# Hybrid diffusion layer on one core: query evictions by pairs, earlier loads of the cached keys and values, another list of attention stages, and the query norm applied inside the exponential

## The chip, the core and the metric

One core of a Trainium2 chip runs the whole program. The metric is the device time of one execution in microseconds (us). The kernel before takes 767.54 us, the median of three runs (766.51 to 768.29).

## What is computed

One layer of a backbone with two streams: 512 latent tokens (four tiles of 128) and 128 context tokens (a fifth tile). Everything is float32; an accurate product is made of three passes on rounded high and low parts.

```python
h = _rms(x, norm_mix) * (1 + sc1) + sh1            # adaLN from SiLU(cond) @ w_ada
q, k, v, gb, gc, u = split(h @ w_in)               # 8 query heads, 2 key heads, head_dim 64
q = _rms(q, q_norm); k = _rms(k, k_norm)           # per head
# latent tokens: rotary on q and k, keys = cached context keys + latent keys (640)
sc = einsum("bqkgd,btkd->bkgqt", q, k) * HEAD_DIM ** -0.5
attn = softmax(sc) @ v
y_conv = gb * conv3(gc * u)
x = x + g1 * (concat(_rms(attn), _rms(y_conv)) @ w_out)
x = x + g2 * ((silu(gate) * up) @ w_down)          # adaLN, then SwiGLU
```

## The kernel before, in words

The program has four stretches. In the first (to about 62 us) the inputs are normalised and transposed, the modulation is computed, and the query columns of the projection are accumulated for all five token tiles in five PSUM banks. In the second (to about 263 us) keys and values are projected and normalised, attention runs, and the convolution mixer is computed as filler between the steps of attention. The third is the output projection, the fourth (from about 335 us) the feed-forward network.

TensorE runs in the order in which the code is written. That order comes from two lists of short words. `P1SEQ` is the first stretch: `d8` is eight throw-away 128x128 matmuls (`spin`, L509) that only keep TensorE busy, `r`/`s`/`x` are norm, scale and transposes of an input tile, `q70` adds step 7, the last, of the query projection for tile 0, `E0` is the eviction of that tile's accumulator by ScalarE (`q_evict`, L581; tile 4, the context, by VectorE). Within `P1SEQ` the other engines also run in written order, with their priorities. Two query tiles share one PSUM tile of two banks: 0 and 1 the first, 2 and 3 the second. A write of the second half waits for any read of the first half that was written before it in the program.

`SEQ` is the second stretch. `k1` is the key/value projection of tile 1 with its head norm, `K1` the transposes of the keys, `c0`/`C0` the same for the cached keys and values (they need no projection), `q0`/`Q0` head norm and transposes of the queries, `a0`/`t0`/`o0` scores and softmax, transposes, and output of the context tile's head group 0, `S5.1` the scores and softmax of the second head of unit 5 (a unit is one latent tile, one key head and one pair of its query heads; 16 units, 32 head-scores), `T5.0` transposes of its probabilities, `O5.0` the product with the values, and `F1` one step of the convolution filler: 9, 9 and 6 matmuls of 320 columns in turn (L703 to L705), sometimes a step of the modulation (L387). The other engines' order in this stretch is set by a scheduler with priorities; within an engine it is strict.

The head norm of queries (`head_norm`, L605) squares (ScalarE L610), sums (VectorE L612), raises to the power -1/2 on GpSimd (L164), multiplies the factor by 1/8 on VectorE (L166), applies gain and rotary (L617 to L628), and multiplies the 512 columns by the factor (L629). The split into a high part (ScalarE L674) and a low part (VectorE L675) comes after that.

A head-score (`att_s`, L811): four matmuls of 320 columns into the only scores tile in PSUM (L817), the negated row maximum on VectorE (L821), the exponential with that maximum as its bias and the row sum as second output on ScalarE (L825), then reciprocal (L828) and scaling by VectorE (L832) or ScalarE (L830). The next head-score can't start before the exponential has read the tile. `ctx_s` (L890) does four heads of the context tile at once.

The loads of the first stretch are issued by SyncE in the order of the string `LOADS`: `x` an input tile, `A` three steps of modulation weights, `W` a block of the projection's weights. The loads of the cached keys and values, `ck` and `cv` (L366, L367), stand behind all of them. The weights rotate through three buffers, so SyncE waits for a buffer in the middle of the list.

Of the kernel before, what the change touches and what calls it, by code (L numbers as in the profile page):

```python
# [9 lines left out]
F32 = mybir.dt.float32  # L10
F32R = mybir.dt.float32r
AF = mybir.ActivationFunctionType
ALU = mybir.AluOpType
AX = mybir.AxisListType

P = 128
# [3 lines left out]
NT = 5  # L20
TOK = NT * P
CTX = 4
HD = 64
NH = 8
NKV = 2
GRP = NH // NKV
# [3 lines left out]
NKEY = 640  # L30
EPS = 1e-6
CG = 32
P1SEQ = ('d8 r0 s0 x0 r1 s1 r2 e00d x1 s2 e01d r3 v0 d4 x2 s3 e20a a0 e10d b0 e11d e21d x3 m0 d4 w e30a h00y l n0 '
# [4 lines left out]
XB = 3  # L38
SEQ = ('k1 c0 q4 k4 C0 k0 K4 F1 Q4 q0 a0 F1 k2 a1 K0 t0 k3 t1 o0 K1 F1 Q0 o1 F1 K2 F1 K3 F1 F1 S0.0 F1 S0.1 '
# [10 lines left out]
GCUT = [0, 6, 12, 17, 22]  # L50
GB = 3
SOP = [20, 0]
# [31 lines left out]
AHEAD = 3  # L84
OSQ = 2
AFB = 4
LOADS = 'xxxxAWxAAWAAWAAAWWWWW'
O_Q, O_K, O_GB, O_GC, O_U = 0, 512, 768, 1280, 1792


def build(ctx, tc, x_prompt, x_sample, c, cache_k, cache_v, c_ctx, norm_mix, norm_ffn, w_ada, b_ada,
# [27 lines left out]
    def T(tag, shape, dt=F32, bufs=1):  # L119
        seq[0] += 1  # L120
        return pools[where.get(tag, "A")][1].tile(list(shape), dt, tag=tag, bufs=bufs, name=f"{tag}_{seq[0]}")
# [33 lines left out]
        pe.matmul(out, lh, rl, start=False, stop=False, skip_group_check=more)  # L155
        pe.matmul(out, ll, rh, start=False, stop=stop, skip_group_check=more)  # L156

    def rstd_of(ss, n, scale, extra=None, tag="rs"):

        w = ss.shape[1]  # L160
        ms = T("ms", (P, w), F32, 4)
        dve.tensor_scalar(ms, ss, scale, EPS, ALU.mult, ALU.add)
        r = T(tag, (P, w), F32, 6)
        pool.tensor_tensor(r, ms, neghalf[:, :w], ALU.pow)  # L164
        if extra is not None:
            dve.tensor_scalar_mul(r, r, extra)  # L166
        return r

    open_pool("A", "left", "")
# [81 lines left out]
    def load_next(later=False):  # L251
        load(order[stream_at[0]], later)
        stream_at[0] += 1
# [104 lines left out]
    for a in LOADS:  # L358
        if a == "A":
            ada1_next(3)  # L360
        elif a == "W":
            load_next(True)
        else:
            x_load()
    ck, cv = (T(x, (P, NKV, HD)) for x in ("ck", "cv"))
    sp.dma_start(ck, cache_k[0, 0])  # L366
    sp.dma_start(cv, cache_v[0, 0])  # L367
    ones = T("ones", (P, P))
    dve.memset(ones, 1.0)
    neghalf = T("neghalf", (P, 16))  # L370
# [214 lines left out]
             "n": h_rest, "E": q_evict, "R": lambda i: rope_tables()}  # L585
    in_pre[0] = True
    for x in P1SEQ.split():
        k = int(x[1:2] or 0)
        if x[0] == "h":
            h_do(k, int(x[2]), len(x) > 3)  # L590
        elif x[0] == "q":
            q_mm(k, int(x[2]))
        elif x[0] == "e":
            xT_evict(k, int(x[2]), x[3])
        else:
            steps[x[0]](k)
# [5 lines left out]
    close_pool("psum")  # L602
    open_psum("pp2", {"t": PT, "c": 5 - PT, "o": 1, "s": 1})

    def head_norm(ps, nh, t, which):  # L605

        w = nh * HD
        p3 = ps.rearrange("p (h d) -> p h d", d=HD)
        sq = T("ph", (P, 512), F32, PHB)[:, :w]
        act.activation(sq, ps, AF.Square)  # L610
        ss = T("hq_ss", (P, NH), F32, 2)[:, :nh]
        dve.tensor_reduce(ss, sq.rearrange("p (h d) -> p h d", d=HD), AX.X, ALU.add)  # L612
        r = rstd_of(ss, nh, 1.0 / HD, HD ** -0.5 if which == 0 else None)
        m1 = T("pr", (P, 512), F32, PRB)[:, :w]
        m13 = m1.rearrange("p (h d) -> p h d", d=HD)
        if t == CTX:
            dve.tensor_tensor(m13, p3, gains[which].unsqueeze(1).to_broadcast([P, nh, HD]), ALU.mult)  # L617
        else:
            cg, sg = tabs[which]
            dve.tensor_tensor(m13, p3, cg[:, t].unsqueeze(1).to_broadcast([P, nh, HD]), ALU.mult)  # L620
            m2 = T("pl", (P, 512), F32, PHB)[:, :w]
            p5 = ps.rearrange("p (h a b c) -> p h a b c", a=2, b=2, c=16)
            m5 = m2.rearrange("p (h a b c) -> p h a b c", a=2, b=2, c=16)
            s5 = sg[:, t].rearrange("p (a b c) -> p a b c", a=2, b=2)
            for b in range(2):
                dve.tensor_tensor(m5[:, :, :, b], p5[:, :, :, 1 - b],
                                  s5[:, :, b].unsqueeze(1).to_broadcast([P, nh, 2, 16]), ALU.mult)
            dve.tensor_tensor(m1, m1, m2, ALU.add)  # L628
        dve.tensor_tensor(m13, m13, r.unsqueeze(2).to_broadcast([P, nh, HD]), ALU.mult)  # L629
        return m13  # L630

# [151 lines left out]
    rB = [None] * NT  # L783
# [27 lines left out]
    def att_s(u, h):  # L811
        t, v, p = u[0:3]
        q = qT[t][:, v * GRP + 2 * p + h, :]
        s2 = PS2()
        for i, kk in enumerate((KA, KB)):
            for g in range(2):
                pe.matmul(s2[:, g, :320], q, kk[:, v, P + g * 320:P + (g + 1) * 320], start=(i == 0), stop=(i == 1))  # L817
        s_in = s2[:, :, :320]
        nm = T("nm", (P, 1), F32, 4)
        with early(SOON):  # L820
            dve.tensor_reduce(nm, s_in, AX.XY, ALU.max, negate=True)  # L821
        pr = T("pr", (P, NKEY), F32, PRB)
        sm = T("sm", (P, 1), F32, 4)
        with early(SOON):
            act.activation(pr.rearrange("p (a b) -> p a b", a=2), s_in, AF.Exp, bias=nm, accum_out=sm)  # L825
        rsm = T("rsm", (P, 1), F32, 4)
        with early(SOON):
            dve.reciprocal(rsm, sm)  # L828
            if NA[h]:
                act.activation(pr, pr, AF.Copy, scale=rsm)  # L830
            else:
                dve.tensor_scalar_mul(pr, pr, rsm)  # L832
        u[3].append(pr)
# [56 lines left out]
    def ctx_s(v):  # L890
# [7 lines left out]
        pr = T("pr", (P, NKEY), F32, PRB)[:, :512].rearrange("p (h k) -> p h k", k=P)  # L898
        with early(SOON):
            dve.tensor_reduce(nm, s3, AX.X, ALU.max, negate=True)  # L900
            for h in range(GRP):
                act.activation(pr[:, h], s3[:, h], AF.Exp, bias=nm[:, h:h + 1], accum_out=sm[:, h:h + 1])
            dve.reciprocal(rsm, sm)
            dve.tensor_tensor(pr, pr, rsm.unsqueeze(2).to_broadcast([P, GRP, P]), ALU.mult)
        cu[v] = pr
# [444 lines left out]
```

## Time and profile before

| | |
|---|---|
| median of three runs | 767.54 us |
| the profiled execution's own time | 768.41 us |
| its span, first to last instruction | 766.6 us |
| TensorE matmul busy | 746.0 us (97%) |
| VectorE busy | 554.0 us (72%) |
| ScalarE busy | 368.2 us (48%) |
| GpSimd busy | 43.7 us (6%) |

How to read it: PE is TensorE's matmul row, PEld its weight loads, DVE VectorE, ACT ScalarE, POOL GpSimd, SP SyncE with its DMA queue. In a timeline row stand the start and the duration in us, the engine, the line, the operation, output <- input by the program's names, and in brackets the idle time of that engine just before and what ended it. The ends of matmuls are modelled, so back-to-back matmuls overlap in the rows and their distance from start to start is what one costs. PEclk is the granted share of TensorE's clock in a stretch.

### The profile page before, as it was taken

The page shows a single profiled execution, that of the slowest core. Times are in us where ns is not written, and L with a number is a line of the kernel's source. Part 1 is how long each engine was busy: PE and PEld are TensorE (multiplying, and loading weights), DVE is VectorE, ACT ScalarE, POOL GpSimd, SP SyncE. Part 2 cuts the span into 40 slices and gives each one's busy share as a digit, 9 for nine tenths or more (in the row PEclk, how much of TensorE's full clock was granted, in tenths as well). Part 3 has the DMA queues.
Part 4 walks back from the last instruction along what each step waited for, and adds up shares of the span by engine and source line. Part 5 has one row for each costly group of instructions (what it writes and reads, how often), then busy time and mean ns, then how long its engine had stood idle before and what let it go on. Part 6 is the DMA issues. An engine that isn't in the chain of part 4 may idle for free.

```text
span 766.6 us, 11914 instructions
## 1 busy us (share of the span) xinstructions
PE 746.0 (97%) x4612; PEld 668.3 (87%) x4612; DVE 554.0 (72%) x1005; ACT 368.2 (48%) x713; POOL 43.7 (6%) x75
## 2 busy tenths in 40 slices
PE   7998989999999999999899999999999999999997
PEld 6677878889999887899898789998889998899986
DVE  5656876785665798779979778884577866778653
ACT  5355756666555634675552225553125541255410
POOL 2402200111000110100000000000000000000000
PEclk9999999999999999999999999999999999999999
DMA  9985133432342364030245313133113232222312
GB/s 290 288 232 158 40 113 110 150 94 90 110 152 88 127 227 137 1 111 28 84 120 169 109 56 109 57 111 110 56 55 91 76 111 71 67 84 83 110 56 82
DMA packets 101390, 84.52 MB, mean 110 GB/s; under 512 B 3503, under 2 KB 81651, under 8 KB 101333
## 3 DMA queue, kind: packets, MB, share of 16 engines
q1 hardware_dynamic: 100980, 83.39, 35.4%
q0 software_dynamic: 352, 0.37, 0.3%
q8 instruction: 36, 0.59, 0.3%
q14 instruction: 22, 0.17, 0.1%
HBM read 79.68 MB, written 2.75 MB: 108 GB/s over the span
## 4 chain that ended last, share of the span: by engine, by line
PE 83%; DVE 7%; ACT 4%; DMA 3%; issue 2%; POOL 1%; SPq 0%; DVEq 0%; POOLq 0%
PE pf L156 17%; PE pf L155 17%; PE pf L154 17%; PE pc L703 3%; PE pc L704 3%; PE pc L705 3%; PE po L860 3%; PE ph L154 2%; PE ph L156 2%; PE ph L155 2%; PE ps L817 2%; PE pc L387 2%; PE pt L843 2%; DMA es<-t 1%; PE ps L154 1%
## 5 line engine op out<-in xcount | busy, mean ns | idle before, releaser
L150 ACT ACTIVATE wh<-wf 128x512 fp32r<-128x512 f32 (+1 forms) x68 | 55.6, 818 | 81.5 <-PE pf L156 69.4
L156 PE MATMUL pf<-wh,gT 128*128 128x512 f32 (+1 forms) x225 | 88.3, 393 | 0.0
L155 PE MATMUL pf<-wl,gT 128*128 128x512 f32 (+1 forms) x225 | 87.7, 390 | 0.0
L154 PE MATMUL pf<-wh,gT 128*128 128x512 f32 (+1 forms) x225 | 87.6, 389 | 0.0
L703 PE MATMUL pc<-hH,wh 128*128 128x320 f32 x192 | 62.1, 323 | 0.4 <-ACT g L766 0.2
L705 PE MATMUL pc<-hH,wl 128*128 128x320 f32 x192 | 60.1, 313 | 0.0
L704 PE MATMUL pc<-hL,wh 128*128 128x320 f32 x192 | 59.9, 312 | 0.0
L151 DVE TENSOR_TENSOR wl<-wf,wh 128x1024 fp32r<-128x1024 f32 (+1 forms) x34 | 39.4, 1159 | 27.0 <-ACT wh L150 22.1
L155 PEld LDWEIGHTS pf<-wl,gT 128*128 128x128 f32 x225 | 42.2, 188 | 10.3 <-issue 0.2
L154 PEld LDWEIGHTS pf<-wh,gT 128*128 128x128 f32 x225 | 42.2, 188 | 9.9 <-ACT wh L150 0.2
L154 PE MATMUL pf<-T,wh 128*128 128x320 f32 x160 | 49.6, 310 | 1.1 <-ACT p L1180 0.6
L156 PEld LDWEIGHTS pf<-wh,gT 128*128 128x128 f32 x225 | 42.3, 188 | 9.3
L156 PE MATMUL pf<-T,wh 128*128 128x320 f32 x160 | 49.4, 309 | 0.0
L154 PE MATMUL pf<-T,wl 128*128 128x320 f32 x160 | 49.4, 309 | 0.0
L155 PE MATMUL pf<-T,wl 128*128 128x320 f32 x160 | 49.4, 309 | 0.0
L155 PE MATMUL pf<-T,wh 128*128 128x320 f32 x160 | 49.4, 309 | 0.0
L156 PE MATMUL pf<-T,wl 128*128 128x320 f32 x160 | 49.4, 309 | 0.0
L154 PE MATMUL pf<-B,wl 128*128 128x320 f32 x152 | 47.1, 310 | 0.0
L156 PE MATMUL pf<-B,wl 128*128 128x320 f32 x152 | 47.0, 309 | 0.0
L155 PE MATMUL pf<-B,wl 128*128 128x320 f32 x152 | 46.9, 309 | 0.0
L1259 DVE TENSOR_TENSOR dm<-pf,g 128x512 f32<-128x512 f32 (+1 forms) x41 | 27.7, 676 | 23.6 <-PE pf L156 23.5
L154 PE MATMUL pf<-B,wh 128*128 128x320 f32 x136 | 42.2, 310 | 1.5 <-DVE cu L1209 1.5
(304 smaller groups left out, 2051.3 us busy)
## 6 DMA issues: line engine op xcount, KB each, us to landing
wf<-in_w_gate_up_dram SPq DMA_DIRECT2D x44, 512.0 KB, 3.9
aw<-in_w_ada_dram SPq DMA_DIRECT2D x24, 512.0 KB, 4.1
wf<-in_w_down_dram SPq DMA_DIRECT2D x20, 512.0 KB, 3.3
wf<-in_w_in_dram SPq DMA_DIRECT2D x18, 512.0 KB, 5.2
af<-in_w_ada_dram SPq DMA_DIRECT2D x32, 256.0 KB, 6.6
x<-in_x_sample_dram SPq DMA_DIRECT2D x8, 512.0 KB, 5.7
wf<-in_w_out_dram SPq DMA_DIRECT2D x8, 512.0 KB, 4.1
wf<-in_w_ada_dram SPq DMA_DIRECT2D x8, 512.0 KB, 3.7
```

What stands on the lines that cost most here:

```text
L150: act.activation(hi, src, AF.Copy)
L151: dve.tensor_tensor(lo, src, f32(hi), ALU.subtract)
L154: pe.matmul(out, lh, rh, start=start, stop=False, skip_group_check=more)
L155: pe.matmul(out, lh, rl, start=False, stop=False, skip_group_check=more)
L156: pe.matmul(out, ll, rh, start=False, stop=stop, skip_group_check=more)
L387: pe.matmul(out[CG * g:CG * (g + 1)], cp[:, k], w, start=(k < 4), stop=(k >= KD - 4), skip_group_check=True)
L703: pe.matmul(acc, wh[:, k], hH[k][:, c0:c0 + n], start=(k == 0), stop=False)
L704: pe.matmul(acc, wh[:, k], hL[k][:, c0:c0 + n], start=False, stop=False)
L705: pe.matmul(acc, wl[:, k], hH[k][:, c0:c0 + n], start=False, stop=(k == KD - 1))
L817: pe.matmul(s2[:, g, :320], q, kk[:, v, P + g * 320:P + (g + 1) * 320], start=(i == 0), stop=(i == 1))
L860: pe.matmul(ov, w, x[:, i].rearrange("p a q -> p (a q)"), start=(g == 0 and i == 0 and n == 0), stop=(last and i == len(kts) - 1 and n == 1))
L1259: dve.tensor_tensor(dm, ps[:, :n], g2[cc][:, oc], ALU.mult)
```

## The change

1. The first word `d8` of `P1SEQ` becomes `d11`.
2. Evictions by pairs: two query accumulations, then their two evictions.
3. `ck` and `cv` are issued behind the fourth block of projection weights instead of behind the eighth.
4. The query norm factor is no longer multiplied into the query. The scores are taken with the unnormalised query (gain and rotary applied), and the exponential gets the factor as its scale. The 1/8 goes into the mean and the epsilon (`scale * by`, `EPS * by` with `by` = 64). The row maximum has to be multiplied by the factor too: one ScalarE copy of 128x1 for each head-score, one VectorE product of 128x4 for each context group. The factors of a tile live in `rq`.
5. Another `SEQ`: three of the fillers in front of the first head-score move, one to behind it and two to behind units 9 and 14. Words and their number are the same (84 fillers); the order of the other words is the same.

```diff
-P1SEQ = ('d8 r0 s0 x0 r1 s1 r2 e00d x1 s2 e01d r3 v0 d4 x2 s3 e20a a0 e10d b0 e11d e21d x3 m0 d4 w e30a h00y l n0 '
+P1SEQ = ('d11 r0 s0 x0 r1 s1 r2 e00d x1 s2 e01d r3 v0 d4 x2 s3 e20a a0 e10d b0 e11d e21d x3 m0 d4 w e30a h00y l n0 '
...
-         'm7 h70 h71 q60 q61 w l q62 q63 q64 w l q70 E0 q71 E1 q72 E2 q73 E3 q74 E4 w l')
+         'm7 h70 h71 q60 q61 w l q62 q63 q64 w l q70 q71 E0 E1 q72 q73 E2 E3 q74 E4 w l')
...
-SEQ = ('k1 c0 q4 k4 C0 k0 K4 F1 Q4 q0 a0 F1 k2 a1 K0 t0 k3 t1 o0 K1 F1 Q0 o1 F1 K2 F1 K3 F1 F1 S0.0 F1 S0.1 '
+SEQ = ('k1 c0 q4 k4 C0 k0 K4 Q4 q0 a0 F1 k2 a1 K0 t0 k3 t1 o0 K1 F1 Q0 o1 K2 F1 K3 F1 S0.0 F1 F1 S0.1 '
...
-LOADS = 'xxxxAWxAAWAAWAAAWWWWW'
+LOADS = 'xxxxAWxAAWAAWAAAWCWWWW'
...
-    def rstd_of(ss, n, scale, extra=None, tag="rs"):
+    def rstd_of(ss, n, scale, by=1.0, tag="rs"):
...
-        dve.tensor_scalar(ms, ss, scale, EPS, ALU.mult, ALU.add)
-        r = T(tag, (P, w), F32, 6)
+        dve.tensor_scalar(ms, ss, scale * by, EPS * by, ALU.mult, ALU.add)
+        r = T(tag, (P, w), F32, {"rB": 1, "rs": 6}.get(tag, NT))
         pool.tensor_tensor(r, ms, neghalf[:, :w], ALU.pow)
-        if extra is not None:
-            dve.tensor_scalar_mul(r, r, extra)
...
+        elif a == "C":
+            ck, cv = (T(n, (P, NKV, HD)) for n in ("ck", "cv"))
+            sp.dma_start(ck, cache_k[0, 0])
+            sp.dma_start(cv, cache_v[0, 0])
...
-        r = rstd_of(ss, nh, 1.0 / HD, HD ** -0.5 if which == 0 else None)
+        r = rstd_of(ss, nh, 1.0 / HD, *((HD, "rq") if which == 0 else ()))
...
+        if which == 0:
+            rq[t] = r
+            return m13
         dve.tensor_tensor(m13, m13, r.unsqueeze(2).to_broadcast([P, nh, HD]), ALU.mult)
...
-            dve.tensor_reduce(nm, s_in, AX.XY, ALU.max, negate=True)
+            dve.tensor_reduce(nm[:, 0:1], s_in, AX.XY, ALU.max, negate=True)
+            act.activation(nm[:, 1:2], nm[:, 0:1], AF.Copy, scale=rs)
...
-            act.activation(pr.rearrange("p (a b) -> p a b", a=2), s_in, AF.Exp, bias=nm, accum_out=sm)
+            act.activation(pr.rearrange("p (a b) -> p a b", a=2), s_in, AF.Exp, bias=nm[:, 1:2], scale=rs, accum_out=sm)
...
+            rs = rq[CTX][:, v * GRP:(v + 1) * GRP]
+            dve.tensor_tensor(nm, nm, rs, ALU.mult)
             for h in range(GRP):
-                act.activation(pr[:, h], s3[:, h], AF.Exp, bias=nm[:, h:h + 1], accum_out=sm[:, h:h + 1])
+                act.activation(pr[:, h], s3[:, h], AF.Exp, bias=nm[:, h:h + 1], scale=rs[:, h:h + 1], accum_out=sm[:, h:h + 1])
```

In the rows below a name with a number behind it is one buffer; line numbers of the changed kernel are up to 8 higher. ScalarE at the end of the first stretch, before: `wh` is a block of weights being rounded, `of` an evicted query tile, `VS` the cached values being rounded.

```order
L528 ACTIVATE wh_674<-wf_165 128x1024
L581 ACTIVATE of_681<-ps_343 128x512
L150 ACTIVATE VS_718<-cv_170 128x2x64
L581 ACTIVATE of_686<-ps_343 128x512
L581 ACTIVATE of_691<-ps_344 128x512
L581 ACTIVATE of_696<-ps_344 128x512
```

ScalarE at the same place after the change:

```order
L527 ACTIVATE wh_677<-wf_169 128x1024
L150 ACTIVATE VS_721<-cv_162 128x2x64
L580 ACTIVATE of_687<-ps_346 128x512
L580 ACTIVATE of_689<-ps_346 128x512
L580 ACTIVATE of_697<-ps_347 128x512
L580 ACTIVATE of_699<-ps_347 128x512
```

The rounding of the cached values stands ahead of the four evictions now, and no longer between the first and the second. VectorE around the first head-score, before: `KB` are transposed keys, `of` sums of the context tile's attention output that wait for a DMA into `es`, `wl` the low part of a weight block, `nm` the row maximum.

```order
L650 CAST KB_717<-pt_1194 128x2x128
L881 TENSOR_TENSOR of_1121<-t_269_1158,es_1160 64x256
L882 TENSOR_TENSOR of_1121<-t_269_1158,es_1160 64x256
L151 TENSOR_TENSOR wl_1643<-wf_1640,wh_1642 128x1024
L821 TENSOR_REDUCE nm_1228<-ps_1223 128x1
L151 TENSOR_TENSOR m_174_724<-of_1121,m_173_723 128x256
```

VectorE at the same place after the change:

```order
L654 CAST KB_720<-pt_1176 128x2x128
L151 TENSOR_TENSOR m_174_727<-of_1113,m_173_726 128x256
L151 TENSOR_TENSOR wl_1484<-wf_1481,wh_1483 128x1024
L826 TENSOR_REDUCE nm_1198<-ps_1193 128x1
L887 TENSOR_TENSOR of_1113<-t_269_1152,es_1154 64x256
L888 TENSOR_TENSOR of_1113<-t_269_1152,es_1154 64x256
```

A weight block's low part still stands directly ahead of the first row maximum; the sums that wait for the second DMA stand behind it now. ScalarE around the first two head-scores, before:

```order
L649 ACTIVATE KA_716<-pt_1194 128x2x128
L150 ACTIVATE wh_1642<-wf_1640 128x1024
L883 ACTIVATE osq_1122<-of_1121 128x256
L150 ACTIVATE m_173_723<-of_1121 128x256
L717 ACTIVATE c_211_900<-pc_1168 128x320
L825 ACTIVATE pr_1230,sm_1231<-ps_1223,nm_1228 128x640
L825 ACTIVATE pr_1258,sm_1259<-ps_1251,nm_1256 128x640
L830 ACTIVATE pr_1258<-pr_1258,rsm_1261 128x640
```

ScalarE at the same place after the change, with the factor `rq` as a new operand:

```order
L653 ACTIVATE KA_719<-pt_1176 128x2x128
L889 ACTIVATE osq_1114<-of_1113 128x256
L150 ACTIVATE m_173_726<-of_1113 128x256
L827 ACTIVATE nm_1198<-nm_1198,rq_920 128x1
L831 ACTIVATE pr_1201,sm_1202<-ps_1193,nm_1198,rq_920 128x640
L889 ACTIVATE osq_1114<-of_1113 128x256
L150 ACTIVATE m_173_726<-of_1113 128x256
L721 ACTIVATE c_226_952<-pc_1183 128x320
L150 ACTIVATE wh_1678<-wf_1676 128x1024
L827 ACTIVATE nm_1228<-nm_1228,rq_920 128x1
L831 ACTIVATE pr_1231,sm_1232<-ps_1223,nm_1228,rq_920 128x640
```

Each exponential has a 128x1 copy of the maximum ahead of it, and the weight block's rounding moved from ahead of the first exponential to between the first and the second. On TensorE the first and the second head-score had one filler of 9 matmuls between them, and have two now, of 9 and 6.

More of the change, by code (lines that the diff above doesn't have):

```diff
@@ L362, in build @@
             load_next(True)
+        elif a == "C":
+            ck, cv = (T(n, (P, NKV, HD)) for n in ("ck", "cv"))
+            sp.dma_start(ck, cache_k[0, 0])
+            sp.dma_start(cv, cache_v[0, 0])
         else:
             x_load()
-    ck, cv = (T(x, (P, NKV, HD)) for x in ("ck", "cv"))
-    sp.dma_start(ck, cache_k[0, 0])
-    sp.dma_start(cv, cache_v[0, 0])
     ones = T("ones", (P, P))
@@ L587, in build @@
     for x in P1SEQ.split():
-        k = int(x[1:2] or 0)
+        k = int(x[1:] if x[0] == "d" else x[1:2] or 0)
         if x[0] == "h":
@@ L603, in build @@
     open_psum("pp2", {"t": PT, "c": 5 - PT, "o": 1, "s": 1})
+    rq = [None] * NT
     def head_norm(ps, nh, t, which):
@@ L818, in att_s @@
         s_in = s2[:, :, :320]
-        nm = T("nm", (P, 1), F32, 4)
+        nm = T("nm", (P, 2), F32, 4)
+        rs = rq[t][:, v * GRP + 2 * p + h:v * GRP + 2 * p + h + 1]
         with early(SOON):
-            dve.tensor_reduce(nm, s_in, AX.XY, ALU.max, negate=True)
+            dve.tensor_reduce(nm[:, 0:1], s_in, AX.XY, ALU.max, negate=True)
+            act.activation(nm[:, 1:2], nm[:, 0:1], AF.Copy, scale=rs)
         pr = T("pr", (P, NKEY), F32, PRB)
```

4 rows, old and new, of the table SEQ are left out of this document.

## The prediction

> **What bounds the kernel.** I read the page first: its totals and the chain that ended last.
>
> ```profile
> span 766.6 us, 11914 instructions
> PE 746.0 (97%) x4612; PEld 668.3 (87%) x4612; DVE 554.0 (72%) x1005; ACT 368.2 (48%) x713; POOL 43.7 (6%) x75
> PE 83%; DVE 7%; ACT 4%; DMA 3%; issue 2%; POOL 1%; SPq 0%; DVEq 0%; POOLq 0%
> ```
>
> TensorE is the bound, and the change adds only three short matmuls to it. So it can gain only where TensorE stands still or runs slowly, and lose only by new waits. The second view is the list of TensorE's waits (total us, times, longest):
>
> ```profile
> PE ps L817 <- ACT pr L825: 2.6, 2, 2.1
> PE ps L154 <- ACT of L581: 1.5, 2, 0.8
> PE pf L154 <- DVE cu L1209: 1.5, 1, 1.5
> PE po L860 <- ACT t L867: 1.2, 1, 1.2
> PE pt L683 <- DVE pl L151: 0.7, 1, 0.7
> PE pt L647 <- ACT osq L639: 0.6, 2, 0.3
> ```
>
> The first, second and last lines are what the change touches; L1209 lies in the feed-forward network, which it leaves alone. The third view is a table of stretches (us; busy time of PE, PEld, DVE, ACT, POOL; granted clock; DMA):
>
> ```profile
> 60.98:64.40 3.42, 3.42 (x23) 3.15 (x24) 1.32 (x2) 1.66 (x2) 0.00 (x0) 1.00 0.96 306
> 98.00:101.20 3.20, 1.14 (x9) 0.98 (x7) 2.39 (x6) 1.22 (x4) 0.00 (x0) 1.00 1.05 368
> 101.20:104.60 3.40, 3.40 (x15) 3.40 (x14) 2.09 (x4) 1.71 (x3) 0.00 (x0) 0.50 0.66 187
> 104.60:110.00 5.40, 4.81 (x34) 4.32 (x34) 4.84 (x9) 2.75 (x6) 0.00 (x0) 1.00 0.00 0
> 120.00:270.00 150.00, 147.55 (x1051) 132.72 (x1050) 99.76 (x198) 91.66 (x186) 13.65 (x24) 1.00 0.36 115
> ```
>
> Around 100 us TensorE waits 2 us for the first exponential, and then runs 3.4 us at half clock: a loss of 1.7 us that no wait shows. Later, in most of the attention (last row), it is busy for 147.55 of 150 us, so little is left to win there.
>
> **The start (d11).** TensorE's weight-load rows: eight spins, then two input tiles' transposes, later a third's.
>
> ```profile
> 3.21 3.78 PE L509 MATMUL pc<-ident 128*128 128x128 f32 x16
> 7.76 1.57 PEld L454 LDWEIGHTS ps<-ident,x 128*128 128x128 f32 x8 [1.07 <-DVE x L493]
> 9.54 1.57 PEld L454 LDWEIGHTS ps<-ident,x 128*128 128x128 f32 x8 [0.21 <-DVE x L493]
> 12.95 0.91 PEld L454 LDWEIGHTS ps<-ident,x 128*128 128x128 f32 x8
> ```
>
> A spin costs 3.78/8 = 0.47 us, so eleven end at 3.21 + 5.2 = 8.4 us, 0.65 past the time when the first tile is ready (7.76). The same eight transposes take 1.57 us here and 0.91 at 12.95: the clock rises in between. If it still rises as late, the later gaps swallow part of the delay and +0.6 is the worst. If the longer unbroken stretch of spins lets it rise before these transposes, two tiles gain 0.66 each: 0.65 - 1.32 = -0.7, and up to -1.1 with the spins behind them. I take -0.2. [...]
>
> **Evictions by pairs, and the cached values sooner.** TensorE, ScalarE, and the piece of the chain of waits with the DMA:
>
> ```profile
> 58.49 0.50 PE L154 MATMUL ps<-wh,hH 128*128 128x512 f32 x1 [0.69 <-ACT of L581]
> 60.98 0.50 PE L154 MATMUL ps<-wh,hH 128*128 128x512 f32 x1 [0.83 <-ACT of L581]
> 57.84 0.60 ACT L581 ACTIVATE of<-ps 128x512 f32<-128x512 f32 x1
> 59.64 0.31 ACT L150 ACTIVATE VS<-cv 128x128 fp32r<-128x128 f32 x1 [1.21 <-DMA cv<-in_cache_v_dram]
> 54.82 4.80 DMA cv<-in_cache_v_dram
> ```
>
> SyncE's queue (five weight blocks in the first row):
>
> ```profile
> 43.27 10.88 SPq L224 DMA_DIRECT2D wf<-in_w_in_dram  x5
> 54.20 0.57 SPq L366 DMA_DIRECT2D ck<-in_cache_k_dram  x1
> ```
>
> Tile 1's accumulation waits for tile 0's eviction, since both share a PSUM tile; tile 3's waits for tile 2's, which stands in ScalarE's queue behind the rounding of `cv`, whose DMA lands at 59.62 (54.82 + 4.80). In pairs, no accumulation stands behind an eviction of its own tile. Both waits go: 0.69 + 0.83, and the refill behind each (0.50 us against 0.40 for a matmul in a stream, by the next row of the same timeline) another 0.1: -1.7. What comes next, the keys' projection, writes another bank, and its weights are rounded before the first eviction at 57.84; so nothing is late there, and -1.5 to -1.8 holds it. `cv` must land ahead of the first eviction now: four of the five blocks that were issued from 43.27 on stand behind it now, so it is issued some 8 us sooner, and it does. The two loads hold SyncE's queue for 0.57 us and about as much again (their issues), hidden as long as those blocks are needed 10 us later.
>
> **Keys, and the context tile.** On VectorE the query factor's scaling waited for GpSimd, with the next key norm queued behind it:
>
> ```profile
> 70.06 0.17 DVE L166 TENSOR_SCALAR rs<-rs 128x8 f32<-128x8 f32 x1 [0.87 <-POOL rs L164]
> 70.34 0.68 DVE L629 TENSOR_TENSOR pr<-pr,rs 128x512 f32<-128x512 f32 x1
> 72.77 0.86 PE L647 MATMUL pt<-identr,osq 128*128 128x128 f32 x4 [0.25 <-ACT osq L639]
> 76.01 0.39 PE L894 MATMUL ps<-KA,qT 128*128 128x256 f32 x1 [0.35 <-ACT qT L684]
> 86.20 0.63 PE L910 MATMUL pt<-ident,pr 128*128 128x128 f32 x4 [0.28 <-DVE pr L904]
> ```
>
> Both rows at the top go (five such multiplications of 0.68 us in all), so the context keys' chain is 0.9 us shorter than the 0.25 us that TensorE waits at 72.77, and with the wait inside that group 0.4 is won. The filler that stood ahead of `Q4` covered the query's eviction; without it the wait at 76.01 grows by some 0.1. The context softmax gets one more small VectorE step and a scale operand in four exponentials, some 0.3 on the wait at 86.20. Against that, a longer filler falls ahead of `Q0`: -0.2. Sum -0.2, between -0.9 and +1.0.
>
> **The first head-score.** VectorE, ScalarE and TensorE:
>
> ```profile
> 96.39 0.45 PE L817 MATMUL ps<-KB,qT 128*128 128x320 f32 x2
> 97.28 1.23 DVE L151 TENSOR_TENSOR wl<-wf,wh 128x1024 fp32r<-128x1024 f32 x1
> 98.43 0.82 DVE L821 TENSOR_REDUCE nm<-ps 128x1 f32<-128x640 f32 x1
> 99.28 0.80 ACT L825 ACTIVATE pr<-ps,nm 128x640 f32<-128x640 f32 x1 [0.94 <-DVE nm L821]
> 100.22 0.56 PE L817 MATMUL ps<-KA,qT 128*128 128x320 f32 x2 [2.06 <-ACT pr L825]
> ```
>
> The scores ended at 96.84 (first row); VectorE was busy with a weight block, and the maximum came 1.6 us late. From there: 0.82 + 0.80 + 0.14 of handing over. The list now puts 15 filler matmuls of 0.147 us (from start to start) behind these scores instead of 9: 2.2 us of cover for 1.3. The new chain is longer by 0.43 (next part). If VectorE is as late as before, 1.6 + 1.8 + 0.4 - 2.2 leaves 1.6 of wait; if it is free, none. The weight block still stands right ahead of the maximum, but one of the sums that waited for a DMA does not, so I take 0.9: -1.2. With it goes the half clock, -1.7: the wait of 0.83 at 60.98 was followed by 3.4 us at full clock (1.00 in the first row of the table of stretches), and this one of 2.06 by 3.4 at half. Together -2.9; from -3.7 (no wait) to 0 (the wait and the half clock stay). [...]
>
> **The 31 other head-scores.** What a per-partition operand costs ScalarE, by groups (count, then busy us and mean ns):
>
> ```profile
> L902 ACT ACTIVATE pr<-ps,nm 128x128 f32<-128x128 f32 x8 | 2.8, 369 | 1.0 <-DVE nm L900 1.0
> L995 ACT ACTIVATE gT<-pt,modB,modA 128x128 f32<-128x128 f32 x40 | 15.2, 466 | 9.7 <-PE pt L987 9.7
> L333 ACT ACTIVATE warm<-warm 128x1 f32<-128x1 f32 x1 | 0.2, 203 | 0.0
> PEld ps L817 <- ACT pr L825: 3.6, 4, 2.3
> 107.64 0.56 PE L817 MATMUL ps<-KA,qT 128*128 128x320 f32 x2 [0.50 <-ACT pr L825]
> ```
>
> One operand more (bias and scale, L995, against bias alone) is 97 ns on a 128x128 tile, so each exponential grows by 0.10. The copy of the maximum is a 128x1 ScalarE operation, 0.20, with a scale operand 0.30, and stands between maximum and exponential, plus 0.03 of handing over. That is 0.43 us for each of 32 chains, 13.8 us in all. Behind the copy wait its own exponential and whatever ScalarE has next, and TensorE's next scores wait for them. Most of it is covered by fillers: TensorE's queue waited for an exponential at 4 places, the first of which is the case above. Three others pay in full, 1.3, and I add 0.2 for those that were just in time: +1.5. Some pairs have 9 matmuls between them where 6 stood, which takes it down to -0.5 with the wait of 1.2 at L867 gone; nine paying places make +4.
>
> **Sum**, on the profiled execution's own 768.41 us (span 766.6; 0.87 above the median of the runs): -0.2 - 1.7 - 0.2 - 2.9 + 1.5 = -3.5, so 764.9 us. About 0.2%, 1.5 us, can be told from no change, so the borders to the median 767.54 are 766.0 and 769.1.
>
> **Rivals.** (1) The softmax chain becomes the bound: with 0.43 us at the 32 copies, the change turns slower than 769.1 once 14 of them pay in full (763.4 without that term, plus 14 x 0.43 = 6.0), at 20 of them 772.0. For it speaks that the older list's fillers were not spaced for this chain, and that most pairs have only 1.8 to 3 us of matmuls between them; against it that TensorE waited at 4 of them. 0.13. (2) The first exponential stays late: VectorE reaches its maximum behind the same weight block, TensorE waits about 2 us and the half clock stays. 768.41 - 0.2 - 1.7 - 0.2 + 1.5 = 767.8. For it speaks the order on VectorE, against it the second filler. 0.17. (3) The half clock does not come from this wait and stays though the wait shrinks: -3.5 + 1.7 = -1.8, 766.6. [...] 0.08. My forecast has 0.62, with a range of its own from 761 to 766.
>
> Faster by over 0.2%: 0.58 of the forecast and 0.05 of the second and third, 0.63. Within: 0.04 + 0.18 = 0.22. Slower: 0.13 + 0.02 = 0.15. The range reaches from 761.0 to 769.2; it leaves out the first rival and a little at the low end.
>
> **What would show it.** In the changed kernel's profile no L580 ends a wait of TensorE near 60 us; the context keys' transposes wait for nothing; the second head-score's wait is under 1.2 us and no stretch of the second stage has a clock of 0.50; exponentials of 640 columns take about 0.89 us, and the copy 0.3; waits of scores for exponentials sum to 2 to 3 us. The prediction is wrong if half clock shows anywhere after 13 us, or if those waits are above 6 us.

## The result, and the profile after

The changed kernel takes 761.88 us (median of 4 runs, 761.28 to 762.14) against 767.59 us before: a ratio of 0.9926, 95% interval 0.9909 to 0.9943, 5.7 us faster. The profiled execution took 762.14 us with a span of 760.4. The forecast of 764.9 had the sign, and the range (761.0 to 769.2) holds the time. The gain is larger than worked out: 6.2 us of span where the sum of the prediction had 3.5.

The changed kernel's page, totals and chain of waits:

```profile
span 760.4 us, 11953 instructions
PE 743.1 (98%) x4618; PEld 665.9 (88%) x4618; DVE 552.1 (73%) x997; ACT 378.5 (50%) x745; POOL 43.2 (6%) x75
PE 83%; DVE 8%; ACT 5%; DMA 2%; issue 1%; POOL 0%; SPq 0%; ACTq 0%; DVEq 0%
```

The top of its list of TensorE's waits, in total us, times and longest, without one of 3.2 us ahead of the first matmul:

```profile
PE ps L821 <- ACT pr L831: 2.1, 3, 0.9
PE pf L154 <- DVE cu L1217: 1.5, 1, 1.5
PE pt L687 <- ACT qT L688: 1.0, 1, 1.0
PE pt L918 <- ACT wh L150: 0.7, 1, 0.7
PE po L866 <- DVE pl L151: 0.5, 1, 0.5
```

Neither an eviction (L580) nor the copy of the attention output (L867 before, L873 now) ends a wait any more, and the longest wait of scores for an exponential is 0.9 where it was 2.1. New is 1.0 at the query transposes L687. Its table of stretches, in the same columns as before:

```profile
57.91:61.33 3.42, 3.42 (x24) 3.14 (x23) 2.45 (x4) 2.94 (x6) 0.00 (x0) 1.00 1.06 354
93.02:96.43 3.41, 2.52 (x17) 1.49 (x18) 2.66 (x6) 3.37 (x8) 0.00 (x0) 1.00 0.50 145
96.43:99.84 3.41, 3.29 (x23) 2.94 (x21) 3.32 (x6) 2.68 (x6) 0.00 (x0) 1.00 0.84 266
114.00:264.00 150.00, 148.60 (x1055) 133.32 (x1053) 98.93 (x195) 99.94 (x213) 12.79 (x24) 1.00 0.37 118
```

There is no stretch of half clock behind the first head-score. In 150 us of attention ScalarE is busy 8 us longer than in the 150 us of the prediction's table (99.94 against 91.66), TensorE 1 us.

Where the 6.2 us of span came from is best read from TensorE's own timeline: its work is the same and nearly in the same order, so the start of the same instruction in both traces gives the lead of the changed kernel at that point. Between the places at which the list moves fillers, the two kernels have done a different number of them. The last column, the net lead, takes those out, at 0.147 us for a matmul of 320 columns and 1.0 for a modulation step of eight matmuls.

| the same instruction | before | after | lead | less fillers not yet done | net lead |
|---|---|---|---|---|---|
| first product of the projection | 18.07 | 17.32 | 0.75 | 0 | 0.75 |
| last step of query tile 3 | 60.98 | 57.91 | 3.07 | 0 | 3.07 |
| scores of the first head-score | 95.99 | 90.05 | 5.94 | 15 x 0.147 + 1.0 | 2.7 |
| scores of the third | 104.64 | 97.10 | 7.54 | 15 x 0.147 | 5.3 |
| scores of the last | 246.59 | 240.37 | 6.22 | 9 x 0.147 | 4.9 |
| first product of the output projection | 263.20 | 257.98 | 5.22 | 0 | 5.2 |
| the end | 766.6 | 760.4 | 6.2 | 0 | 6.2 |

So the start gave 0.75, the road to the last evictions 2.3, the context tile took 0.4, the first two head-scores gave 2.6, the other thirty nothing, and the output projection and the network 1.0. The rows behind the first entries, weight loads and matmuls at the start:

```profile
7.89 0.91 PEld L453 LDWEIGHTS ps<-ident,x 128*128 128x128 f32 x8
9.48 0.86 PEld L453 LDWEIGHTS ps<-ident,x 128*128 128x128 f32 x8 [0.68 <-DVE x L492]
17.32 0.49 PE L154 MATMUL ps<-wh,hH 128*128 128x512 f32 x1 [0.62 <-ACT hH L471]
57.91 0.40 PE L154 MATMUL ps<-wh,hH 128*128 128x512 f32 x1
```

The first tiles' transposes take 0.91 and 0.86 where they took 1.57 each, and the last step of tile 3 starts without a wait. ScalarE at the evictions:

```profile
57.66 0.29 ACT L150 ACTIVATE VS<-cv 128x128 fp32r<-128x128 f32 x1
57.86 2.04 ACT L580 ACTIVATE of<-ps 128x512 f32<-128x512 f32 x4
```

All four evictions run in one piece behind the cached values, which have landed. The first head-score, on VectorE, ScalarE and TensorE:

```profile
90.50 1.22 DVE L151 TENSOR_TENSOR wl<-wf,wh 128x1024 fp32r<-128x1024 f32 x1
91.64 0.82 DVE L826 TENSOR_REDUCE nm<-ps 128x1 f32<-128x640 f32 x1
92.55 0.30 ACT L827 ACTIVATE nm<-nm,rq 128x1 f32<-128x1 f32 x1 [2.66 <-DVE nm L826]
92.88 0.88 ACT L831 ACTIVATE pr<-ps,nm,rq 128x640 f32<-128x640 f32 x1
93.91 0.55 PE L821 MATMUL ps<-KA,qT 128*128 128x320 f32 x2 [0.91 <-ACT pr L831]
```

From the end of the maximum (92.46) to the end of the exponential (93.76) it is 1.30 us where it was 0.83. By groups, all 32:

```profile
L831 ACT ACTIVATE pr<-ps,nm,rq 128x640 f32<-128x640 f32 x32 | 28.3, 884 | 0.6
L827 ACT ACTIVATE nm<-nm,rq 128x1 f32<-128x1 f32 x32 | 9.3, 290 | 16.0 <-DVE nm L826 15.8
```

and before:

```profile
L825 ACT ACTIVATE pr<-ps,nm 128x640 f32<-128x640 f32 x32 | 25.4, 794 | 20.4 <-DVE nm L821 20.2
```

The single operations cost what was forecast: 0.09 more for the exponential, 0.29 for the copy.

### The profile page after: what moved, and what is told of

Same layout as the page of the kernel before. It is cut to its first block, busy times and chain, and to the rows that moved or that the text cites. A ratio compares the mean times of both kernels' runs of the same rounds, so it can differ in the third digit from the quotient of the medians.

```text
span 760.4 us, 11953 instructions
## 1 busy us (share of the span) xinstructions
PE 743.1 (98%) x4618; PEld 665.9 (88%) x4618; DVE 552.1 (73%) x997; ACT 378.5 (50%) x745; POOL 43.2 (6%) x75
## 4 chain that ended last, share of the span: by engine, by line
PE 83%; DVE 8%; ACT 5%; DMA 2%; issue 1%; POOL 0%; SPq 0%; ACTq 0%; DVEq 0%
PE pf L154 17%; PE pf L156 17%; PE pf L155 17%; PE pc L707 3%; PE pc L709 3%; PE pc L708 3%; PE pc L386 2%; PE ph L154 2%; PE ph L156 2%; PE ph L155 2%; PE po L866 2%; PE ps L821 2%; PE pt L849 2%; PE ps L154 1%; DMA es<-t 1%
## 5 line engine op out<-in xcount | busy, mean ns | idle before, releaser
L154 PE MATMUL pf<-wh,gT 128*128 128x512 f32 (+1 forms) x225 | 88.1, 392 | 0.0
L154 PEld LDWEIGHTS pf<-wh,gT 128*128 128x128 f32 x225 | 42.2, 188 | 9.9 <-ACT wh L150 0.2
L154 PE MATMUL pf<-T,wh 128*128 128x320 f32 x160 | 49.4, 309 | 0.5 <-ACT u L1188 0.5
L154 PE MATMUL pf<-T,wl 128*128 128x320 f32 x160 | 49.3, 308 | 0.0
L154 PE MATMUL pf<-B,wl 128*128 128x320 f32 x152 | 47.1, 310 | 0.0
L154 PE MATMUL pf<-B,wh 128*128 128x320 f32 x136 | 42.1, 310 | 1.5 <-DVE cu L1217 1.5
```

What stands on the lines that cost most here:

```text
L154: pe.matmul(out, lh, rh, start=start, stop=False, skip_group_check=more)
```

## The experiments

There are twelve kernels, and their times are medians. "Alone" means on the kernel before. The changed kernel has only the four runs of the result. The kernel before was run again beside each group of experiments, at 768.26, 768.37 and 768.37 us where it had 767.59 beside the changed kernel, so a difference of under about 1 us to the changed kernel's 761.88 says little.

**Evictions by pairs and sooner load, alone.**

```diff
-'... q70 E0 q71 E1 q72 E2 q73 E3 q74 E4 w l'   LOADS = 'xxxxAWxAAWAAWAAAWWWWW'
+'... q70 q71 E0 E1 q72 q73 E2 E3 q74 E4 w l'   LOADS = 'xxxxAWxAAWAAWAAAWCWWWW'
```

> The kernel before with the evictions by pairs and the sooner load alone. Theory (the gains add up): TensorE's lead at the end of the first stretch, about 2.0 us as in the changed kernel's trace, stays to the end: 765.6 us, ratio 0.9974. Rival (given back): the first row maximum stands behind a weight block on VectorE whose time is set by its load, so TensorE arrives sooner and waits longer, 2.06 us becoming 3 to 4 us, and the time is 767 to 767.6.

765.23 against 768.26: ratio 0.9962 (0.9949 to 0.9976). The lead stays. The wait for the first exponential is 1.83 us here, not 3, so nothing was given back. Not all of the 3.0 us need be the evictions': no half clock follows that wait in this profile (mean granted clock 1.0), and three of these twelve runs have a mean granted clock under 0.999, against eight of the eighteen of the kernel before beside them.

**The list alone.**

```diff
-... K4 F1 Q4 ... Q0 o1 F1 K2 F1 K3 F1 F1 S0.0 F1 S0.1 ... T9.1 F1 F1 O9.0 ... T14.1 F1 F1 T14.2 ...
+... K4 Q4 ... Q0 o1 K2 F1 K3 F1 S0.0 F1 F1 S0.1 ... T9.1 F1 F1 F1 O9.0 ... T14.1 F1 F1 F1 T14.2 ...
```

> The kernel before with the other list of stages alone. Theory: the second filler covers the first exponential, the wait of 2.06 us falls under 1.2, no stretch at half clock, less 0.65 us lost at the query transposes Q4: -2.0, 765.6 us. Rival 1: VectorE's weight block is as late in absolute time, the wait stays near 2 us and the half clock with it: 767 to 768. Rival 2 (half clock has another cause): the wait shrinks and the half clock stays, 767.3.

763.02 against 768.26: ratio 0.9932 (0.9907 to 0.9957), 5.2 us, far over the 2.0 of the theory. Its waits:

```profile
PE ps L154 <- ACT of L581: 2.8, 2, 2.1
PE ps L817 <- ACT pr L825: 0.8, 1, 0.8
PE pt L683 <- ACT qT L684: 0.7, 1, 0.7
```

One wait of 0.8 for an exponential is left of 2.6, and the waits at L860 are gone from the top of the list. The evictions cost 2.8 in this execution where the profile of before had 1.5. Followed as in the table above, its net lead over the kernel before is -1.1 us at the first head-score, 1.5 at the third and 5.4 at the last. The place where I looked for the list's gain gave 2.6, and the 3.9 behind it are the larger part.

**The factor in the exponential alone** (item 4 of the change on the kernel before, list and loads untouched).

> The kernel before with the query factor in the exponential alone. Theory (the copies are covered): 0.43 us more in each of 32 chains, but TensorE pays under 0.5 us for it, and the key norm's wait at 72.8 us goes (0.4): 767.3, same within 0.2%. Rival (the copies pay, the list of the whole change saves them): with fillers where they stood, at least eight places pay 0.2 to 0.4 us: 769 or more.

772.73 against 768.26: ratio 1.006 (1.0038 to 1.0082). It is slower, as the rival said. Its scores' waits:

```profile
PE ps L820 <- ACT pr L830: 5.5, 6, 2.4
```

**All but the factor in the exponential** (the changed kernel with item 4 taken back).

> The changed kernel with the query factor multiplied into the query as before (longer start, pairs, sooner load and list kept). Theory (copies covered, their price 0 to +0.5, and the key norm's wait back): 761.5 to 762.5, same as the changed kernel. Rival (copies cost about the 1.5 us of the prediction, and something else of the change gained more): 760.4 or less.

758.73 against 768.26: ratio 0.9871 (0.9849 to 0.9894). It is 3.2 us faster than the changed kernel, so the theory that the copies are covered falls. This version computes the softmax as before and beats both kernels.

**The old list in the changed kernel** (`SEQ` of before).

> The changed kernel with the list of stages of before. Theory (a wait of about 2 us at the second head-score brings the half clock): the wait is 1.8 to 2.5 us again, 3.4 us follow at half clock, in all +2.5: 764.4 us. Rival (half clock has another cause): the wait is back without half clock, or half clock without it: 762.7 to 763.3.

769.52 against 768.37: ratio 1.0012 (0.9999 to 1.0026), 7.6 us slower than the changed kernel. The half clock came back with its wait of 2.01, as the theory said, but that is only a third of the loss: the changed kernel's net lead over this one is -0.7 us at the first head-score, 1.9 at the third and 7.6 at the output projection. With the copies in the chain the old list pays at many places.

**The copy twice.**

```diff
+            act.activation(nm[:, 2:3], nm[:, 0:1], AF.Copy, scale=rs)
             act.activation(nm[:, 1:2], nm[:, 0:1], AF.Copy, scale=rs)
```

> The changed kernel with the copy of the row maximum made twice in each of the 32 chains (0.3 to 0.4 us more each). Theory (the 0.43 us were free because most chains had that much slack, and at 12 of 32 places the scores now start 0.14 us behind the exponential, so the slack is used up): these 12 pay in full, +3.5 to +5: 765.4 to 767. Rival (chains have slack to spare): under +1: 762 to 762.8.

764.76 against 768.37: ratio 0.9957 (0.9944 to 0.997), 2.9 us over the changed kernel, between the two theories and nearer to the one in which the slack is used up. The second copy lengthens the way from maximum to exponential by 0.21 us on the mean (below), and 13 places at 0.21 are 2.7.

**Eight spins in the changed kernel** (`d11` back to `d8`).

> The changed kernel with eight spins instead of eleven. Theory: the clock rises some 5 us later, the first product of the projection starts 0.75 us later and that stays: 762.6 us. Rival (a later wait swallows it): 761.9.

761.71 against 768.37: ratio 0.992 (0.9908 to 0.9932), the same as the changed kernel, as the rival said. Its first transposes:

```profile
8.10 0.86 PEld L453 LDWEIGHTS ps<-ident,x 128*128 128x128 f32 x8 [1.44 <-DVE ms L162]
```

Here eight spins were enough for the full rate. In the kernel with the pairs alone they were not:

```profile
7.93 3.28 PEld L455 LDWEIGHTS ps<-ident,x 128*128 128x128 f32 x16 [1.05 <-DVE ms L162]
```

Of the six profiles with eight spins three have these transposes at full rate and three at the slow one; of the eight with eleven spins all have the full rate.

**One filler put back ahead of the context's query transposes**, taken from behind unit 9.

```diff
-... K4 Q4 q0 ... T9.1 F1 F1 F1 O9.0 ...
+... K4 F1 Q4 q0 ... T9.1 F1 F1 O9.0 ...
```

> The changed kernel with one filler put back ahead of the context's query transposes (taken from behind unit 9, where three stood). Theory: the wait of 1.0 us at these transposes goes and what follows keeps it: 761.1 us. Rival (the context's softmax chain is bound by ScalarE and VectorE, the wait moves to the next transposes or to the first head-score): 761.9 or slower, and if that wait passes 2 us the half clock comes back, 764.

771.22 against 768.37: ratio 1.0026 (1.001 to 1.0042), 9.3 us slower than the changed kernel. Eight of its twelve runs have a mean clock of 0.998 or less; the other four have a median of 768.6, so without half clock it is 6.7 us slower. The wait at Q4 went as expected, and neither theory saw the rest:

```profile
PE ps L821 <- ACT pr L831: 5.8, 6, 1.9
PE ps L821 <- DVE KB L654: 1.0, 1, 1.0
```

Between the two places every later filler step falls one step sooner in the list, and the scores wait 5.8 us for exponentials where they waited 2.1.

**The product on VectorE.**

```diff
-            act.activation(nm[:, 1:2], nm[:, 0:1], AF.Copy, scale=rs)
+            dve.tensor_tensor(nm[:, 1:2], nm[:, 0:1], rs, ALU.mult)
```

> The changed kernel with the product of the row maximum and the factor made by VectorE right behind the maximum, in place of ScalarE's copy. Theory 1 (the 3 us by which the factor in the exponential costs are delay of the chain: from the end of the maximum to the start of the exponential 0.64 us on the mean against 0.16): a 128x1 operation of VectorE with its hand-over is about 0.2, half of the delay goes: 760.2 to 761. Theory 2 (the loss is not in these chains but at the context tile and in the order of the other work): 761.9, same as the changed kernel.

762.35 against 768.37: ratio 0.9922 (0.99 to 0.9943), the same as the changed kernel. The operation is half as long:

```profile
L827 DVE TENSOR_TENSOR nm<-nm,rq 128x1 f32<-128x1 f32 x32 | 5.0, 155 | 0.5
```

But in 16 of 32 chains VectorE's queue has something else between the maximum and the product:

```profile
102.56 0.68 DVE L151 TENSOR_TENSOR pl<-pt,ph 128x512 fp32r<-128x512 f32 x1
103.15 0.15 DVE L827 TENSOR_TENSOR nm<-nm,rq 128x1 f32<-128x1 f32 x1
```

So the exponential starts 0.65 us behind the maximum on the mean, as with ScalarE's copy (0.64). My estimate of the delay was wrong. The time did not move where the delay did not move, which agrees with the delay being the price but does not prove it.

**No product** (a constant bias, the maximum still waited for).

```diff
-            act.activation(pr..., s_in, AF.Exp, bias=nm[:, 1:2], scale=rs, accum_out=sm)
+            act.activation(pr..., s_in, AF.Exp, bias=shift, scale=rs, accum_out=sm)
```

> The changed kernel with no product at all in the 32 head-scores: the exponential still waits for the row maximum, but takes a constant of -40 as its bias, so the shift of the softmax is not the row maximum here. The exponential keeps both operands. Theory 1 (delay): only the 0.1 us of the second operand is left of the delay: 759 to 759.8. Theory 2 (loss elsewhere): 761.3 or more.

754.57 against 768.37: ratio 0.9825 (0.9803 to 0.9847), 7.3 us under the changed kernel and so more than the product can cost by theory 1. The traces divide it: between the third head-score and the output projection it gains 2.9 us on the changed kernel, and from there to the end, where the two programs are the same, another 4.7 (1.7 went the other way, to waits for loads in the first stretch of this execution). The down projection's matmuls, in this kernel:

```profile
L154 PE MATMUL pf<-wh,gT 128*128 128x512 f32 (+1 forms) x225 | 86.9, 386 | 0.0
```

and in the changed kernel:

```profile
L154 PE MATMUL pf<-wh,gT 128*128 128x512 f32 (+1 forms) x225 | 88.1, 392 | 0.0
```

From start to start they are 0.222 us apart on the mean here and 0.228 there. So about 3 us are the product's price, and the rest is not evidence on it.

**The list's fillers moved to the first head-score only.**

```diff
-... K4 F1 Q4 ... Q0 o1 F1 K2 F1 K3 F1 F1 S0.0 F1 S0.1 ...
+... K4 Q4 ... Q0 o1 K2 F1 K3 F1 S0.0 F1 F1 F1 F1 S0.1 ...
```

> The kernel before with the three fillers of the list moved to behind the first head-score, so that from the second head-score on every filler step falls where it did before (the other list lets two steps fall later until unit 14). Theory 1 (the list gains by cover at the first head-score alone, wait and half clock): as the whole other list, 762.5 to 763.5, or better. Theory 2 (a good part comes from where the filler steps and their follow-ups on ScalarE fall in units 0 to 9): the first wait goes, but the waits at 107 and 147 us (0.5 and 1.24) stay: 765 to 766.

769.0 against 768.37: ratio 1.0009 (0.999 to 1.0027), no gain at all, which neither theory gave. The wait at the second head-score is gone (the third now waits 0.8), and the net lead over the kernel before is 1.7 us at the third head-score and 1.8 at the last; under the whole list it was 1.5 and 5.4. Two of its waits:

```profile
145.29 0.38 PE L860 MATMUL po<-ph,VS 128*128 128x256 f32 x1 [1.24 <-ACT t L867]
263.52 0.50 PE L154 MATMUL ph<-wh,m 128*128 128x512 f32 x1 [1.93 <-ACT rs L758]
```

The first is the 1.24 us that the kernel before has at 147, kept as theory 2 said. The second is new and gives the lead back: the first product of the output projection waits until ScalarE has read the filler's last PSUM tile (L758), which in the kernel before it did not wait for. So at the first head-scores this list gains what the whole list gains there (from -1.1 to 1.7), and nothing behind them.

**No row maximum and no product** (a constant bias).

```diff
-            dve.tensor_reduce(nm[:, 0:1], s_in, AX.XY, ALU.max, negate=True)
-            act.activation(nm[:, 1:2], nm[:, 0:1], AF.Copy, scale=rs)
```

> The changed kernel without row maximum and product in the 32 head-scores: the exponential takes a constant of -40 as its bias, so the shift of the softmax is not the row maximum here. The chain is shorter than before the change by 0.8 us. Theory 1 (the chains' delay is what TensorE pays): no scores wait for an exponential any more: 757 to 758.5. Theory 2 (the waits of the context tile and the order of the other work hold the time): 759.5 to 761.

752.81 against 768.37: ratio 0.9797 (0.9776 to 0.9819). No scores wait for an exponential. From the third head-score to the output projection it gains 4.2 us on the changed kernel, and 4.8 behind it, with matmuls of 0.222 us as in the kernel without the product. Without those 4.8 it would be at 757.6, where theory 1 had it. It is the fastest, but its shift is fixed: it holds only while the scaled scores stay in the range of the exponential.

## Why the prediction was right, and where its terms were not

| term | forecast | measured on the profiles | 
|---|---|---|
| start | -0.2 | -0.75 |
| evictions by pairs, cached values | -1.7 | -2.3, of it 0.4 ahead of the evictions |
| keys and context tile | -0.2 | +0.4 |
| first head-score | -2.9 | -2.6 |
| 31 other head-scores | +1.5 | +0.1, as +4.4 for the factor and about -4.3 for the list |
| behind the attention | 0 | -1.0 |

**The start.** "If the longer unbroken stretch of spins lets it rise before these transposes" is what happened. But the gain depends on the execution: eight spins do it too in three of six profiles (0.86 us for eight transposes, against 1.56 to 1.64 in the other three), and the medians of eight and eleven spins do not differ (761.71 and 761.88). With eleven spins the first eight take 0.86 to 0.91 us in all eight profiles.

**The evictions** were right in mechanism and undersized. On the two profiles the waits of 0.69 and 0.83 are worth 0.96 and 1.09 of lead, so about 0.27 goes with each beyond its idle time, where I took 0.1. And I took the waits of one execution as the price: in the three other profiles that still evict tile by tile they are 2.1 and 0.7 (list alone), 1.9 and 0.7 (list at the first head-score only), 1.7 and 0.7 (factor alone). The bounds of -1.5 to -1.8 left no room for either.

**The context tile.** "Without it the wait at 76.01 grows by some 0.1" failed: the query transposes (L687) now wait 1.0 us for ScalarE, since the filler removed there covered 1.3 us. Putting it back removes that wait and costs more elsewhere. The wait of 0.25 ahead of the context keys' transposes went as written. In the context softmax the factor cost more than the 0.3 I took: where 0.28 was waited at 86.20 there are now 0.41 for an exponential (L910) and 0.70 at L918.

**The first head-score** came out as written: the maximum still stands behind the weight block, the wait is 0.91 (I took 0.9), the half clock is gone.

**The other head-scores** are where two errors cancelled. The step from 0.43 us in each of 32 chains to "Three others pay in full, 1.3" undersized the factor. Worked out from the 32 maxima and exponentials of each trace (mean time from the end of the maximum to the start of the exponential; places where the next scores start within 0.2 us of the exponential's end):

| kernel | maximum to exponential, us | tight places (of 31) | median, us |
|---|---|---|---|
| before | 0.17 | 5 | 767.6 |
| list alone | 0.16 | 4 | 763.0 |
| all but the factor | 0.16 | 4 | 758.7 |
| factor alone | 0.59 | 10 | 772.7 |
| changed kernel, old list | 0.59 | 9 | 769.5 |
| changed kernel | 0.64 | 13 | 761.9 |
| product on VectorE | 0.65 | 10 | 762.4 |
| copy twice | 0.85 | 13 | 764.8 |
| no product | 0.15 | 4 | 754.6 |

A tight place has no slack: in these traces the next scores never start sooner than about 0.14 us behind the exponential. With 0.48 us of delay and 0.09 of longer exponential the tight places go from 4 to 13, and the attention loses 4.4 us against the version without the factor (lead of the one trace over the other at the output projection). I had counted the places that waited before; the ones that matter are those whose slack, beyond these 0.14, is under 0.57. In the trace without the factor these are twelve of 31, and what they lack sums to 4.1 us, or to 2.9 without the two behind the first two head-scores, where the trace with the factor loses only 0.1. So the tight places account for most of the 4.4 us and not for all of it. Only three of the 13 tight places show in the list of waits: the end of a matmul is modelled, so a stall that hides in its tail has no idle time. The scores at 107.79 are such a place. The changed kernel:

```profile
107.07 0.82 PE L849 MATMUL pt<-ident,pr 128*128 128x128 f32 x6
107.79 0.56 PE L821 MATMUL ps<-KA,qT 128*128 128x320 f32 x2
```

and the kernel with all but the factor:

```profile
106.11 0.82 PE L844 MATMUL pt<-ident,pr 128*128 128x128 f32 x6
106.68 0.54 PE L818 MATMUL ps<-KA,qT 128*128 128x320 f32 x2
```

The same six transposes are followed by the scores after 0.57 us there and 0.72 here, 0.15 lost without a bracket.

What paid for it I had not seen at all: I read the list as cover at the first head-score. Moving three fillers also moves every filler step behind them to another place (two steps later until unit 9, one until unit 14), with its ScalarE eviction and its weight block. Of the list's 5.4 us of lead, 3.6 are missing when only the first place is changed, and one step of shift the other way costs the changed kernel 9.3 (6.7 without half clock). Which steps collide with which exponentials was not tried one by one.

**The rivals.** The first, the chain as the bound at 772, is what the factor does alone (772.7); in the whole change the list kept it away. In the second the wait stays near 2 us; it is 0.91, so this rival falls. In the third the half clock has another cause; it falls too: inside the program half clock stood only directly behind the waits of 2.06 and 2.01 us, in the profiles of before and of the old list (mean granted clock 0.998 and 0.997, against 0.999 or 1.0 in the twelve others). But the wait is not enough: one of 2.37 us kept its clock, as the last section shows.

**Behind the attention**, 1.0 us: a wait of 0.57 in the network is gone (L1180). The prediction put this term at nothing. It comes with the factor: from the output projection to the end the five profiles without it take 503.4 to 503.6 us (the kernel with all but the factor among them), and those with it 502.2 to 502.6, or 503.2 with the filler put back, leaving out the two with the constant bias. So of the 4.4 us that the factor costs in the attention 1.0 comes back here, which leaves about the 3.2 us of the medians. How it does so is open, as is the cause of the 4.7 us in the kernel without the product.

## What to carry to other kernels

Fillers in a hand-written list are not only cover: each has follow-ups on other engines, and moving one shifts all behind it (one step back cost 9.3 us here), so a list is judged over its whole length and again after every change of a chain's length. Before lengthening a chain, count the places by their slack, not by the waits that the list shows. And price a small operation that is put between two others by the mean time from its input to its consumer, with what the queues hold in between: here a copy of 0.29 us on ScalarE became 0.48 of delay, and a product of 0.155 us on VectorE the same.

## What the hardware showed that was not expected

**Half clock, and the idle time ahead of it.** Two kernels had a wait of about 2.0 us and half clock behind it (2.06 before, 2.01 here). The kernel with the old list, by stretches of 3.41 us that end where its clock changes:

```profile
93.38:96.79 3.41, 1.40 (x11) 1.14 (x9) 2.31 (x4) 2.28 (x6) 0.00 (x0) 1.00 0.94 281
96.79:100.21 3.42, 3.42 (x13) 3.42 (x14) 2.62 (x5) 1.11 (x3) 0.00 (x0) 0.50 0.86 281
```

The kernel with the factor alone had a longer wait, 2.37 us, and kept its clock:

```profile
95.95:99.36 3.41, 2.02 (x13) 1.76 (x13) 3.13 (x5) 1.39 (x5) 0.00 (x0) 1.00 0.90 267
99.36:102.77 3.41, 2.43 (x16) 2.43 (x17) 2.22 (x5) 1.58 (x4) 0.00 (x0) 1.00 1.01 328
```

The borders of the first table are where the granted clock changes. In the kernel with the factor alone and in the one with the filler put back no clock changes there, and the borders are my estimate: laid back from the drop at the program's end in steps of 3.4133 us. The step is worked out from two traces. In the kernel before, the drop in the attention lasts 3.413 us, and the one at the end of the program comes 665.60 us after it, 195 times 3.4133; in the changed kernel the drop at the end comes 750.93 us after the trace's first clock record, 220 times 3.4133. With these borders the wait in the kernel with the factor alone lies in two stretches, 1.39 us of idle time in one and 0.98 in the other. The kernel with the filler put back has 1.77 idle within one stretch, at full clock:

```profile
113.30:116.72 3.42, 1.65 (x15) 0.86 (x8) 3.04 (x6) 3.42 (x7) 0.00 (x0) 1.00 0.41 95
116.72:120.13 3.41, 3.41 (x29) 3.41 (x28) 1.82 (x4) 2.54 (x6) 0.00 (x0) 1.00 1.03 356
```

So a stretch of 3.41 us with 2.01 us idle was followed by half clock here, and one with 1.77 by full clock. With the whole traces of before and after cut up in the same way, from 20 us on: in the kernel before, half clock stands behind 2.06 us idle and at the end of the program, and full clock behind all other stretches, with 1.47 at most; in the changed kernel the only drop is the one at the end, behind 2.19 us, and the other stretches have 1.46 at most. What comes of idle times between these is not shown.

A stretch of 3.41 us at half clock costs 1.7 us, and the runs of one kernel differ by about as much. Of the 58 runs of the kernel before beside the experiments, 30 had a mean granted clock of 0.998 or less (median 769.4 us) and 28 of 0.999 or more (767.4). No run of the changed kernel, or of those with all but the factor, eight spins, the second copy, the product on VectorE or no maximum, was under 0.999. With the pairs alone three of twelve were, and with the list alone four of six; its profile still has a wait of 2.1 at the evictions. A part of the change's gain is thus that no wait near 2 us is left, which by these counts takes the pairs and the list together, and one profile shows it or doesn't by chance.

**The same matmul is not always equally fast.** At full clock the down projection's 675 matmuls (645 of 512 columns, 30 of 256) start 0.228 us apart on the mean in the other kernels and 0.222 in the two with the constant bias, worth 4 us (the pages' mean of one at L154 is 389 to 392 ns there and 386 here). The cause stays open.
